# RG-LRU's shifted products handed out in finer steps, and the S5 scan started eight steps later, in a hybrid decoder block

## Chip, core and metric

The kernel runs on one core of a Trainium2 chip. The metric is the time of one execution on the device in microseconds. Three runs of the kernel before gave 1511.58, 1511.49 and 1508.52 us (median 1511.49). A fourth execution was profiled; all rows below come from it.

## What is computed

One layer of a decoder on 256 tokens with model width 2048, everything in float32. After an RMS norm one large product `xn @ w_in` feeds three branches that are merged by sigmoid gates, then comes `w_out`, a residual, a second norm, and an MLP of width 8192.

```python
proj = xn @ w_in                                  # 2048 x 11264
u_s5, u_lru, q, k, v, gate_logits = jnp.split(proj, offs, axis=-1)
gates = jax.nn.sigmoid(gate_logits + b_gate)
y_s5   = s5_branch(u_s5, ...)      # complex diagonal scan over time, GELU, GLU
y_lru  = rglru_branch(u_lru, ...)  # causal convolution of width 4, two block gates, real scan over time
y_attn = stick_breaking_attention(q, k, v)
merged = g_s5 * (y_s5 @ w_br_s5) + g_lru * (y_lru @ w_br_lru) + g_attn * (y_attn @ w_br_attn)
h = x + merged @ w_out
h = h + squared(relu(rms(h) @ w_up)) @ w_down;  return rms(h)
```

In the RG-LRU branch the convolution is `xc = b + sum_k x[t-3+k] * w[k]`: one scaled copy and three shifted products. In the S5 branch the complex scan is turned into real ones by rotating with a table of cosines and sines.

## The kernel before

**Units.** All weights (w_in, the three w_br, w_glu, w_out, w_up, w_down) are read once as a stream of 520 units. A unit is two 128x512 float32 pieces, 512 KB. SyncE loads it into a `raw` tile (L130, three buffers). ScalarE casts it to `hi` (L146), VectorE takes `lo = raw - hi` (L147), each with three buffers, and TensorE does three products per piece, hi by hi, lo by hi and hi by lo, so that fp32r products keep the precision. A unit is 12 matmuls of 512 columns in `chunk_tok` (L241 to L243) and `pair_tok`, or 24 of 256 columns in `chunk` (L225 to L227). I number the units from 0, and write cast k, lo k and raw k for the instructions that make unit k's tiles.

`next_unit` issues the loads to unit i+3 and cast and lo of unit i+2 ahead of the matmuls of unit i. With three buffers, cast k can start when unit k-3 has left TensorE, which is when unit k-2 starts there.

**Order of the units.** 0 to 15 and 16 to 31 are w_in for the inputs of RG-LRU and of S5 (24 matmuls each). 32 to 79 are four times eight units of gate columns and four of w_br_lru (from here 12 matmuls). 80 to 127 make k, q and v twice, 128 to 175 are gates and w_br_attn, 176 to 191 gates of S5, then w_glu, w_br_s5 with more gates, w_out, and from unit 264 the MLP.

**Side work.** Everything else (norm, convolution, scans, attention) is written as generators. After each unit's matmuls `pump` adds every task's rate to its credit and runs one step, up to a `yield`, for each whole credit. What a step issues is put in program order behind the casts, los and matmuls so far, on every engine that it uses. `finish(task)` runs a task to its end on the spot; the RG-LRU task is finished ahead of unit 40, the S5 task ahead of the GLU at unit 192.

The names that matter here:
- `lru_half` (L523): for each of its two parts and two channel tiles a scaled copy (L535, ScalarE) and three shifted products (L537, VectorE), then a `yield`; then block products on TensorE (L543, L544), sigmoids (L545, L546), tanh (L550), exp (L555), the root (L563), the scan (L570), and the split of the result (L572, L573). Rate 1.15 steps a unit (L576). `scaled` (L386) makes its inputs, and those of S5.
- `s5_scan` (L631), rate 1.27 (L593), started ahead of unit 32: `s5_tables` (L604 to L611) makes the angles and two sines with a table of ScalarE; `s5_split` (L618 to L623) splits an input tile into `ux`; `s5_stack` (L627) copies it with twelve small DMAs on SyncE's queue, the one on which the weights are loaded; then eight rounds of products (L650), copies (L652), rotations (L660 to L670, L681 to L692) and scans (L705).
- `gates` (L750, L751): VectorE scales the logits, ScalarE takes their sigmoid, which needs another table than the sine.

Of the kernel before, what the change touches and what calls it, by code (L numbers as in the profile page):

```python
# [46 lines left out]
def hybrid_block(ctx: ExitStack, tc: tile.TileContext, io, out):  # L47
# [116 lines left out]
    def later(gens, rate):  # L164
        side.append([deque(gens), rate, 0.0])
        return side[-1]
# [333 lines left out]
    def lru_load():  # L500
        for t, src in ((wr, "lru_w_r"), (wi, "lru_w_i")):
            for h in range(2):
                nc.sync.dma_start(t[h * 64:(h + 1) * 64, :, h * 64:(h + 1) * 64], io[src][h])
                yield

    def lru_params():
        for _ in range(4):
            yield
        lc = const.tile([P, 4, WT], F32, name="lc")
        nc.vector.scalar_tensor_tensor(lc[:, 0, :], lam, -1.0, lam, ALU.mult, ALU.min)  # L510
        nc.scalar.activation(lc[:, 1, :], lc[:, 0, :], AF.Exp)
        nc.scalar.activation(lc[:, 2, :], lc[:, 1, :], AF.Ln, bias=1.0)
        nc.vector.tensor_scalar(lc[:, 3, :], lam, -1.0, 0.0, ALU.mult, ALU.max)
        nc.vector.tensor_tensor(lc[:, 3, :], lc[:, 3, :], lc[:, 2, :], ALU.add)
        nc.vector.tensor_scalar(sp4, lc[:, 3, :], 4.0, None, ALU.mult)
        nc.vector.tensor_scalar(nsp8, lc[:, 3, :], -8.0, None, ALU.mult)
        yield
        yield from lru_load()
# [4 lines left out]
    def lru_half(c, us):  # L523
        parts = []
        for m in range(2):
            if m == 0:
                t = [lp.tile([P, 2, L], F32, tag=n_, name=f"lru_{n_}{c}") for n_ in ("xc", "r", "i", "th")]
            else:
                w4 = [pp.tile([P, 2, 2, L], F32, tag=n_, name=f"lru_{n_}{c}", bufs=2) for n_ in ("tc", "ts")]
                t = [w_[:, k] for w_ in w4 for k in range(2)]  # L530
            cts = [(j, slice(4 * c + 2 * m + j, 4 * c + 2 * m + j + 1)) for j in range(2)]
            parts.append((us[m], cts, *t))
        for u, cts, xc, r, i_, th in parts:
            for j, k in cts:
                nc.scalar.activation(xc[:, j, :], u[:, j, :], AF.Identity, scale=cw[:, 3, k], bias=cb[:, k])  # L535
                for s in range(1, 4):
                    nc.vector.scalar_tensor_tensor(xc[:, j, s:], u[:, j, :L - s], cw[:, 3 - s, k], xc[:, j, s:], ALU.mult, ALU.add)  # L537
                yield
        yield
        for u, cts, xc, r, i_, th in parts:  # L540
            for j, k in cts:
                ps = pss.tile([P, CH], F32, tag="ps", name=f"ps_l{c}_{k.start}")
                nc.tensor.matmul(ps[:, 0:L], wr[:, k.start, :], xc[:, j, :], start=True, stop=True, skip_group_check=True)  # L543
                nc.tensor.matmul(ps[:, L:], wi[:, k.start, :], xc[:, j, :], start=False, stop=True, skip_group_check=True)  # L544
                nc.scalar.activation(r[:, j, :], ps[:, 0:L], AF.Sigmoid, bias=br_[:, k])  # L545
                nc.scalar.activation(i_[:, j, :], ps[:, L:], AF.Sigmoid, bias=bi_[:, k])  # L546
            yield
        for u, cts, xc, r, i_, th in parts:
            for j, k in cts:
                nc.scalar.activation(th[:, j, :], r[:, j, :], AF.Tanh, scale=sp4[:, k])  # L550
            nc.vector.tensor_tensor(i_, i_, xc, ALU.mult)
        yield
        for u, cts, xc, r, i_, th in parts:
            for j, k in cts:
                nc.scalar.activation(r[:, j, :], r[:, j, :], AF.Exp, scale=nsp8[:, k])  # L555
        yield
        for u, cts, xc, r, i_, th in parts:
            nc.vector.scalar_tensor_tensor(th, r, 1.0, th, ALU.add, ALU.mult)
            nc.scalar.activation(r, th, AF.Identity, scale=-1.0, bias=1.0)
            nc.vector.scalar_tensor_tensor(th, r, 1.0, th, ALU.add, ALU.mult)  # L560
        yield
        for u, cts, xc, r, i_, th in parts:
            nc.scalar.activation(th, th, AF.Sqrt, bias=tiny)  # L563
        yield
        for u, cts, xc, r, i_, th in parts:
            nc.vector.tensor_tensor(i_, i_, th, ALU.mult)
        yield
        for u, cts, xc, r, i_, th in parts:
            for j, k in cts:
                nc.vector.tensor_tensor_scan(xc[:, j, :], r[:, j, :], i_[:, j, :], 0.0, ALU.mult, ALU.add)  # L570
            s = slice(cts[0][1].start, cts[0][1].start + 2)
            nc.scalar.copy(ylru_hi[:, s, :], xc)  # L572
            nc.vector.tensor_tensor(ylru_lo[:, s, :], xc, ylru_hi[:, s, :].bitcast(F32), ALU.subtract)  # L573
            yield

    lq = later([lru_params()], 1.15)  # L576
    u_banks = {}

    def lru_in(c):
# [10 lines left out]
    lru_in(1)  # L590


    S5_RATE = 1.27  # L593

    def s5_tables(b):
        c = pp.tile([P, NT, 16, 16], F32, tag="tc", name=f"tc{b}", bufs=2)
# [34 lines left out]
    def s5_scan():  # L631
        v = ypool.tile([P, 2, NT, L], F32, tag="yhi", name="s5_v")
        t12 = ypool.tile([P, 2, NT, L], F32, tag="ylo", name="s5_t")
        vr, vi, t1, t2 = v[:, 0], v[:, 1], t12[:, 0], t12[:, 1]
        tabs, more = s5_tables(0)
        yield from more
        s5_split(0)
        yield
        yield
        for t in range(NT):  # L640
            s5_stack(t)
            yield
        tt = nc.vector.tensor_tensor
        for b in range(WT):
            c, s = tabs
            t3 = pp.tile([P, NT, L], F32, tag="t3", name=f"t3_{b}")
            for t in range(NT):
                ps = pss.tile([P, CH], F32, tag="ps", name=f"ps_v{b}")
                for i in range(2):
                    nc.tensor.matmul(ps[:, i * L:(i + 1) * L], stk[:, t, 1, i * P:(i + 1) * P], stk[:, t, 0, :], start=i == 0, stop=True,  # L650
                                     skip_group_check=True)
                nc.scalar.copy(v[:, :, t, :], v2(ps))  # L652
                if t % 2:
                    yield
            more = iter(())
            if b + 1 < WT:
                s5_split(b + 1)
                tabs, more = s5_tables(b + 1)
                yield
            tt(t1, vr, c, ALU.mult)  # L660
            yield
            tt(t2, vi, s, ALU.mult)
            yield
            tt(t1, t1, t2, ALU.add)
            yield
            tt(t3, vi, c, ALU.mult)
            yield
            tt(vr, vr, s, ALU.mult)
            yield
            tt(t3, t3, vr, ALU.subtract)  # L670
            next(more, None)
            yield
            for x_ in (t1, t3):
                for t in range(NT):
                    j = b * NT + t
                    tt_scan(x_[:, t, :], rad[:, j:j + 1].broadcast_to([P, L]), x_[:, t, :])
                    if b + 1 < WT and x_ is t1:
                        s5_stack(t)
                    yield
            next(more, None)  # L680
            tt(t2, t1, c, ALU.mult)  # L681
            yield
            tt(vr, t3, s, ALU.mult)
            next(more, None)
            yield
            tt(t2, t2, vr, ALU.subtract)
            yield
            tt(vi, t3, c, ALU.mult)
            yield
            tt(t1, t1, s, ALU.mult)  # L690
            yield
            tt(t1, t1, vi, ALU.add)  # L692
            yield
            yield
            ps = pss.tile([P, CH], F32, tag="ps", name=f"ps_y{b}")
            for k, w_ in enumerate((t2, t1)):
                for t in range(NT):
                    nc.tensor.matmul(ps[t * 32:t * 32 + 32, 0:L], ce[:, k, b * NT + t, :, :], w_[:, t, :], start=k == 0, stop=k == 1,
                                     skip_group_check=True, tile_position=(0, t * 32))
            nc.vector.scalar_tensor_tensor(us5[:, b, :], us5[:, b, :], dsk[:, b:b + 1], ps[:, 0:L], ALU.mult, ALU.add)  # L700
            if b % 2:
                gq.append(later([gelu(b)], 1.0))
# [62 lines left out]
    def gate_branch(idx, wname, ys, ready):  # L765
        for c in range(4):
            gts = gates(idx, c, lambda c_, j: tmp.tile([P, 2, L], F32, tag="gate", name=f"gate{idx}_{c_}_{j}", bufs=3))
            finish(ready)
            branch(idx, c, gts, wname, ys)

    sq = later([s5_scan()], S5_RATE)
    gate_branch(1, "w_br_lru", lambda kt: (ylru_hi[:, kt, :], ylru_lo[:, kt, :]), ready=lq)
    lru.close()
# [98 lines left out]
    for q in range(4):  # L872
        s = slice(2 * q, 2 * q + 2)
# [4 lines left out]
    for c in range(2):  # L878
        banks = chunk("w_glu", c, W, lambda kt: (yg_hi[:, kt, :], yg_lo[:, kt, :]))
        for j in range(2):  # L880
# [4 lines left out]
            s = slice(c * 4 + 2 * j, c * 4 + 2 * j + 2)  # L885
# [285 lines left out]
```

## Time and profile before

| what | value |
|---|---|
| median of three runs | 1511.49 us |
| the profiled execution | 1512.1 us |
| its span, first to last instruction | 1510.3 us |
| TensorE (PE) | 1488.4 us busy (99%), 7518 matmuls |
| VectorE (DVE) | 1175.2 us busy (78%) |
| ScalarE (ACT) | 782.3 us busy (52%) |
| mean granted clock of TensorE | 0.995 |
| chain that ended last | PE 83%, DVE 9%, issue 3%, ACT 2%, DMA 2% |

How to read it: the ends of matmuls are modelled, and a matmul of 512 columns is shown for 0.39 us while the next one starts 0.23 us after it. Time that TensorE lost is therefore read from the distance between two starts, not from the busy share.

### The profile page before, as it was taken

What the parts mean: (1) busy time and instruction counts of PE and PEld (TensorE: products, weight loads), DVE (VectorE), ACT (ScalarE), POOL (GpSimd) and SP (SyncE); (2) the same over time, 40 slices, a digit from 0 to 9 for tenths busy, and PEclk for the clock granted to TensorE, in tenths of its full rate; (3) what the DMA queues carried; (4) which work ended last, traced back from release to release, by engine and by line L of the source; (5) the groups of instructions that cost most, each with busy time, mean ns of one, the idle gap of its engine ahead of it and who ended that gap; (6) DMA issues with size and microseconds to landing.
All of it is one profiled execution on the core that took longest, in us unless ns stands there. A gap on an engine that the chain in (4) does not pass through costs nothing.

```text
span 1510.3 us, 19900 instructions
## 1 busy us (share of the span) xinstructions
PE 1488.4 (99%) x7518; PEld 1260.5 (83%) x7518; DVE 1175.2 (78%) x1468; ACT 782.3 (52%) x920; POOL 35.3 (2%) x60
## 2 busy tenths in 40 slices
PE   9999999999999999999999999999999999999997
PEld 9997788989887878988887888888888888888886
DVE  6767998897988989689799796568854787558965
ACT  6767556565765564544455544344433444344443
POOL 1400000000000000000000000000000000000011
PEclk9999999999999999999999999999999999999999
DMA  9546766665555666666855666666666666666664
GB/s 287 157 153 176 228 205 201 187 182 168 175 172 183 208 182 210 189 202 190 276 182 188 197 184 205 194 185 196 198 194 193 193 195 195 195 191 191 192 197 152
DMA packets 89858, 292.41 MB, mean 194 GB/s; under 512 B 12834, under 2 KB 17058, under 8 KB 89634
## 3 DMA queue, kind: packets, MB, share of 16 engines
q1 hardware_dynamic: 89618, 291.07, 62.6%
q8 instruction: 59, 0.97, 0.3%
q14 instruction: 37, 0.30, 0.1%
q10 hardware_dynamic: 144, 0.07, 0.0%
HBM read 282.71 MB, written 2.10 MB: 189 GB/s over the span
## 4 chain that ended last, share of the span: by engine, by line
PE 83%; DVE 9%; issue 3%; ACT 2%; DMA 2%; SPq 0%; DVEq 0%; ACTq 0%
PE mt_w_up L242 6%; PE mt_w_up L241 6%; PE mt_w_up L243 6%; PE mt_w_in L242 5%; PE mt_w_in L243 5%; PE mt_w_in L241 5%; PE mt_w_down L242 4%; PE mt_w_down L241 4%; PE mt_w_down L243 4%; PE mp_w_down L277 4%; PE mp_w_down L278 4%; PE mp_w_down L276 4%; PE mm_w_in L227 4%; PE mm_w_in L225 4%; PE mm_w_in L226 4%; DVE lo L147 3%
## 5 line engine op out<-in xcount | busy, mean ns | idle before, releaser
L146 ACT CAST hi<-raw 128x1024 fp32r<-128x1024 f32 (+1 forms) x521 | 545.2, 1049 | 625.9 <-PE mt_w_up L243 131.4
L147 DVE TENSOR_TENSOR lo<-raw,hi 128x1024 fp32r<-128x1024 f32 (+1 forms) x521 | 637.9, 1225 | 287.7 <-ACT hi L146 284.1
L242 PE MATMUL mt_w_in<-lo,xhi 128*128 128x512 f32 x448 | 176.1, 393 | 3.9 <-DVE lo L147 3.7
L241 PE MATMUL mt_w_in<-hi,xhi 128*128 128x512 f32 x448 | 175.2, 396 | 0.2 <-ACT hi L146 0.2
L243 PE MATMUL mt_w_in<-hi,xlo 128*128 128x512 f32 x448 | 175.2, 391 | 0.0
L241 PE MATMUL mt_w_up<-hi,hhi 128*128 128x512 f32 x448 | 174.3, 389 | 0.0
L242 PE MATMUL mt_w_up<-lo,hhi 128*128 128x512 f32 x448 | 174.3, 389 | 0.0
L243 PE MATMUL mt_w_up<-hi,hlo 128*128 128x512 f32 x448 | 174.3, 389 | 0.0
L227 PE MATMUL mm_w_in<-xhi,lo 128*128 128x256 f32 x512 | 145.4, 286 | 4.5 <-DVE lo L147 4.5
L225 PE MATMUL mm_w_in<-xhi,hi 128*128 128x256 f32 x512 | 146.5, 286 | 0.5 <-ACT hi L146 0.4
L226 PE MATMUL mm_w_in<-xlo,hi 128*128 128x256 f32 x512 | 145.7, 285 | 0.0
L728 DVE STREAM_TRANSPOSE reluT<-relu 32x256 f32<-32x256 f32 x256 | 111.5, 436 | 4.2
L242 PEld LDWEIGHTS mt_w_in<-lo,xhi 128*128 128x128 f32 x448 | 84.6, 189 | 24.0 <-DVE lo L147 7.6
L227 PEld LDWEIGHTS mm_w_in<-xhi,lo 128*128 128x128 f32 x512 | 98.7, 194 | 5.5 <-DVE lo L147 5.5
L242 PE MATMUL mt_w_down<-lo,hd_hi 128*128 128x512 f32 (+1 forms) x272 | 102.5, 377 | 0.0
L241 PE MATMUL mt_w_down<-hi,hd_hi 128*128 128x512 f32 (+1 forms) x272 | 102.4, 377 | 0.0
L243 PE MATMUL mt_w_down<-hi,hd_lo 128*128 128x512 f32 (+1 forms) x272 | 102.4, 376 | 0.0
L225 PEld LDWEIGHTS mm_w_in<-xhi,hi 128*128 128x128 f32 x512 | 99.2, 194 | 1.1 <-ACT hi L146 1.0
L277 PE MATMUL mp_w_down<-lo,hd_hi 128*128 128x512 f32 x256 | 99.8, 390 | 0.1
L278 PE MATMUL mp_w_down<-hi,hd_lo 128*128 128x512 f32 x256 | 99.6, 389 | 0.0
L276 PE MATMUL mp_w_down<-hi,hd_hi 128*128 128x512 f32 x256 | 99.6, 389 | 0.0
L241 PEld LDWEIGHTS mt_w_in<-hi,xhi 128*128 128x128 f32 x448 | 84.5, 189 | 17.8 <-ACT hi L146 0.7
(299 smaller groups left out, 2370.2 us busy)
## 6 DMA issues: line engine op xcount, KB each, us to landing
raw<-in_w_in SPq DMA_DIRECT2D x175, 512.0 KB, 4.3
raw<-in_w_up SPq DMA_DIRECT2D x128, 512.0 KB, 4.2
raw<-in_w_down SPq DMA_DIRECT2D x128, 512.0 KB, 4.2
raw<-in_w_out SPq DMA_DIRECT2D x32, 512.0 KB, 4.2
raw<-in_w_br_lru SPq DMA_DIRECT2D x16, 512.0 KB, 4.6
raw<-in_w_br_attn SPq DMA_DIRECT2D x16, 512.0 KB, 4.1
raw<-in_w_br_s SPq DMA_DIRECT2D x16, 512.0 KB, 4.1
stk<-ux SPq DMA_DIRECT2D x96, 64.0 KB, 4.1
```

The source lines that it names most:

```text
L146: anchor["act"] = nc.scalar.copy(h[:, k, :], r[:, k, :]).ins
L147: anchor["dve"] = nc.vector.tensor_tensor(l_[:, k, :], r[:, k, :], h[:, k, :].bitcast(F32), ALU.subtract).ins
L225: nc.tensor.matmul(o, wh[:, kk, s], xh, start=first and ct % 2 == 0, stop=False, skip_group_check=True)
L226: nc.tensor.matmul(o, wh[:, kk, s], xl, start=False, stop=False, skip_group_check=True)
L227: mm = nc.tensor.matmul(o, wl[:, kk, s], xh, start=False, stop=last and ct % 2 == 1, skip_group_check=True)
L241: nc.tensor.matmul(banks[j], xh[:, s], wh[:, a:b], start=kt == 0, stop=False)
L242: nc.tensor.matmul(banks[j], xh[:, s], wl[:, a:b], start=False, stop=False)
L243: return nc.tensor.matmul(banks[j], xl[:, s], wh[:, a:b], start=False, stop=kt == ng * UK - 1)
L276: nc.tensor.matmul(o, xh[:, s], wh[:, kk, :], start=kt == 0, stop=False)
L277: nc.tensor.matmul(o, xh[:, s], wl[:, kk, :], start=False, stop=False)
L278: mm = nc.tensor.matmul(o, xl[:, s], wh[:, kk, :], start=False, stop=kt == ng * UK - 1)
L728: nc.vector.transpose(d_[32 * a:32 * a + 32, :, :, 32 * b:32 * b + 32], s_[32 * b:32 * b + 32, :, :, 32 * a:32 * a + 32])
```

## The change

```diff
--- before.py
+++ after.py
@@ -535,6 +535,8 @@
                 nc.scalar.activation(xc[:, j, :], u[:, j, :], AF.Identity, scale=cw[:, 3, k], bias=cb[:, k])
                 for s in range(1, 4):
                     nc.vector.scalar_tensor_tensor(xc[:, j, s:], u[:, j, :L - s], cw[:, 3 - s, k], xc[:, j, s:], ALU.mult, ALU.add)
+                    if s == 2:
+                        yield
                 yield
         yield
         for u, cts, xc, r, i_, th in parts:
@@ -573,7 +575,7 @@
             nc.vector.tensor_tensor(ylru_lo[:, s, :], xc, ylru_hi[:, s, :].bitcast(F32), ALU.subtract)
             yield
 
-    lq = later([lru_params()], 1.15)
+    lq = later([lru_params()], 1.45)
     u_banks = {}
 
     def lru_in(c):
@@ -590,7 +592,7 @@
     lru_in(1)
 
 
-    S5_RATE = 1.27
+    S5_RATE = 1.35
 
     def s5_tables(b):
         c = pp.tile([P, NT, 16, 16], F32, tag="tc", name=f"tc{b}", bufs=2)
@@ -632,6 +634,8 @@
         v = ypool.tile([P, 2, NT, L], F32, tag="yhi", name="s5_v")
         t12 = ypool.tile([P, 2, NT, L], F32, tag="ylo", name="s5_t")
         vr, vi, t1, t2 = v[:, 0], v[:, 1], t12[:, 0], t12[:, 1]
+        for _ in range(8):
+            yield
         tabs, more = s5_tables(0)
         yield from more
         s5_split(0)
```

Four things: a second `yield` inside the three shifted products of each of a half's four tiles (after the product with s = 2), so that a half has 18 steps in place of 14; the RG-LRU task's rate 1.45 in place of 1.15; the S5 task's rate 1.35 in place of 1.27; and eight empty steps ahead of the S5 task's first. No arithmetic is added or taken away. Every later step of both tasks falls at another unit. Line numbers after the first edit are 2 higher than before, after the last 4 higher.

VectorE around lo 26 (`lo_1120` before, `lo_1115` after): the last RG-LRU split of the first half, the products of the second (L537), and the scaled inputs of S5 (L386). Before:

```order
L573 TENSOR_TENSOR ylru_lo<-lru_tc_631,ylru_hi 128x512
L537 SCALAR_TENSOR_TENSOR lru_xc_1069<-ulru_817,par,lru_xc_1069 128x255 x2
L537 SCALAR_TENSOR_TENSOR lru_xc_1069<-ulru_817,par,lru_xc_1069 128x254 x2
L537 SCALAR_TENSOR_TENSOR lru_xc_1069<-ulru_817,par,lru_xc_1069 128x253 x2
L386 TENSOR_TENSOR us_99<-mm_w_in_0_16_821,rstd 128x512
L386 TENSOR_TENSOR us_99<-mm_w_in_1_16_822,rstd 128x512
L147 TENSOR_TENSOR lo_1120<-raw_1079,hi_1119 128x1024
```

After:

```order
L575 TENSOR_TENSOR ylru_lo<-lru_tc_631,ylru_hi 128x512
L537 SCALAR_TENSOR_TENSOR lru_xc_1099<-ulru_797,par,lru_xc_1099 128x255
L386 TENSOR_TENSOR us_99<-mm_w_in_0_16_801,rstd 128x512
L537 SCALAR_TENSOR_TENSOR lru_xc_1099<-ulru_797,par,lru_xc_1099 128x254
L386 TENSOR_TENSOR us_99<-mm_w_in_1_16_802,rstd 128x512
L147 TENSOR_TENSOR lo_1115<-raw_1069,hi_1114 128x1024
```

Ahead of lo 26 there were six products, and now there are two; the others stand behind lo 26, 27 and 28.

ScalarE at the S5 task's first sines (`ts`, `tc`), between two casts; before these are cast 37 (`hi_1485`) and cast 38:

```order
L146 CAST hi_1485<-raw_1458 128x1024
L572 CAST ylru_hi<-lru_xc_1069 128x512
L618 CAST ux<-us_99 128x256
L622 ACTIVATE ux<-bco,par 128x2x64
L609 ACTIVATE tc_1431<-ts_1432 128x1024
L622 ACTIVATE ux<-bco,par 128x2x64
L610 ACT_TABLE_LOAD
L610 ACTIVATE ts_1432<-ts_1432 128x1024
L572 CAST ylru_hi<-lru_tc_1073 128x512
L611 ACTIVATE tc_1431<-tc_1431,half_pi 128x1024
L146 CAST hi_1510<-raw_1483 128x1024
```

After, cast 42 (`hi_1581`) and cast 43; `gate_0_0` and `gate_0_1` are the gates of units 32 to 39:

```order
L146 CAST hi_1581<-raw_1551 128x1024
L620 CAST ux<-us_99 128x256
L624 ACTIVATE ux<-bco,par 128x2x64
L611 ACTIVATE tc_1548<-ts_1549 128x1024
L755 ACT_TABLE_LOAD
L755 ACTIVATE gate_0_0_1571<-gate_0_0_1571 128x512
L755 ACTIVATE gate_0_1_1574<-gate_0_1_1574 128x512
L612 ACT_TABLE_LOAD
L612 ACTIVATE ts_1549<-ts_1549 128x1024
L613 ACTIVATE tc_1548<-tc_1548,half_pi 128x1024
L624 ACTIVATE ux<-bco,par 128x2x64
L146 CAST hi_1608<-raw_1579 128x1024
```

The sines moved from unit 37 to unit 42, where the sigmoids of the first gates (L755) now stand among them with a table load of their own; RG-LRU's two casts (L572) are gone from there.

ScalarE at a later round of S5. Before, this stands between cast 150 (`hi_4654`) and cast 151, with the gates of w_br_attn's second chunk:

```order
L146 CAST hi_4654<-raw_4623 128x1024
L609 ACTIVATE tc_4380<-ts_4381 128x1024
L610 ACT_TABLE_LOAD
L610 ACTIVATE ts_4381<-ts_4381 128x1024
L751 ACT_TABLE_LOAD
L751 ACTIVATE gate_1_0_4644<-gate_1_0_4644 128x512
L751 ACTIVATE gate_1_1_4647<-gate_1_1_4647 128x512
L611 ACT_TABLE_LOAD
L611 ACTIVATE tc_4380<-tc_4380,half_pi 128x1024
L146 CAST hi_4676<-raw_4652 128x1024
```

After, between cast 78 (`hi_2420`) and cast 79, with the gates of w_br_lru's fourth chunk:

```order
L146 CAST hi_2420<-raw_2389 128x1024
L611 ACTIVATE tc_2174<-ts_2175 128x1024
L612 ACT_TABLE_LOAD
L612 ACTIVATE ts_2175<-ts_2175 128x1024
L755 ACT_TABLE_LOAD
L755 ACTIVATE gate_3_0_2410<-gate_3_0_2410 128x512
L755 ACTIVATE gate_3_1_2413<-gate_3_1_2413 128x512
L613 ACT_TABLE_LOAD
L613 ACTIVATE tc_2174<-tc_2174,half_pi 128x1024
L146 CAST hi_2442<-raw_2418 128x1024
```

The same ten instructions with three table loads now stand at unit 78. At unit 149 of the kernel after, sine, cosine and gates also meet, in an order with two table loads.

## Rows read from the trace of the kernel before

**Rows 1.** The page: a costly group; one DMA issue (xcount, KB, us to landing).
```profile
L147 DVE TENSOR_TENSOR lo<-raw,hi 128x1024 fp32r<-128x1024 f32 (+1 forms) x521 | 637.9, 1225 | 287.7 <-ACT hi L146 284.1
...
raw<-in_w_in SPq DMA_DIRECT2D x175, 512.0 KB, 4.3
```
**Rows 2.** Timeline of PE in the MLP: start us, us, instruction.
```profile
1200.10 0.39 PE L242 MATMUL mt_w_up<-lo,hhi 128*128 128x512 f32 x1
...
1200.33 0.39 PE L243 MATMUL mt_w_up<-hi,hlo 128*128 128x512 f32 x1
```
**Rows 3.** Timeline of PE: matmuls of units 14, 26, 32, 36, 151 that waited.
```profile
51.63 0.39 PE L227 MATMUL mm_w_in<-xhi,lo 128*128 128x256 f32 x1 [0.44 <-DVE lo L147]
...
92.31 0.42 PE L227 MATMUL mm_w_in<-xhi,lo 128*128 128x256 f32 x1 [1.93 <-DVE lo L147]
...
115.49 0.50 PE L242 MATMUL mt_w_in<-lo,xhi 128*128 128x512 f32 x1 [0.73 <-DVE lo L147]
...
129.18 0.50 PE L242 MATMUL mt_w_in<-lo,xhi 128*128 128x512 f32 x1 [1.91 <-DVE lo L147]
...
484.08 0.73 PE L241 MATMUL mt_w_br_attn<-hi,ya_hi 128*128 128x512 f32 x2 [2.15 <-ACT hi L146]
```
**Rows 4.** Windows: stretch, length, busy of PE, PEld, DVE, ACT, POOL, PEclk, DMA, GB/s.
```profile
92.60:96.00 3.40, 3.40 (x18) 3.40 (x18) 3.40 (x7) 0.00 (x0) 0.00 (x0) 0.51 0.74 182
...
485.10:488.50 3.40, 3.40 (x8) 2.72 (x9) 3.40 (x4) 0.83 (x1) 0.00 (x0) 0.51 0.51 154
1200.00:1203.40 3.40, 3.40 (x17) 2.82 (x16) 2.87 (x5) 1.50 (x2) 0.00 (x0) 1.00 0.65 188
```
**Rows 5.** Timeline of DVE ahead of lo 26.
```profile
84.57 1.27 DVE L570 TENSOR_TENSOR_SCAN lru_tc<-lru_tc,lru_ts 128x256 f32<-128x256 f32 x2
...
86.87 0.69 DVE L573 TENSOR_TENSOR ylru_lo<-lru_tc,ylru_hi 128x512 fp32r<-128x512 f32 x1
87.47 2.45 DVE L537 SCALAR_TENSOR_TENSOR lru_xc<-ulru,par,lru_xc 128x255 f32<-128x255 f32 x6
89.84 1.29 DVE L386 TENSOR_TENSOR us<-mm_w_in,rstd 128x512 f32<-128x512 f32 x2
91.04 1.22 DVE L147 TENSOR_TENSOR lo<-raw,hi 128x1024 fp32r<-128x1024 f32 x1
```
**Rows 6.** Timeline of ACT from cast 150 to cast 151.
```profile
473.81 1.06 ACT L146 CAST hi<-raw 128x1024 fp32r<-128x1024 f32 x1 [0.49 <-PE mt_w_in L243]
474.77 1.05 ACT L609 ACTIVATE tc<-ts 128x1024 f32<-128x1024 f32 x1
475.84 1.28 ACT L610 ACT_TABLE_LOAD   x1
477.13 1.06 ACT L610 ACTIVATE ts<-ts 128x1024 f32<-128x1024 f32 x1
478.20 1.28 ACT L751 ACT_TABLE_LOAD   x1
479.50 1.15 ACT L751 ACTIVATE gate<-gate 128x512 f32<-128x512 f32 x2
480.65 1.28 ACT L611 ACT_TABLE_LOAD   x1
481.95 1.15 ACT L611 ACTIVATE tc<-tc,half_pi 128x1024 f32<-128x1024 f32 x1
483.00 2.92 ACT L146 CAST hi<-raw 128x1024 fp32r<-128x1024 f32 x3
```
**Rows 7.** Timeline of ACT: casts 31 and 32; the first copy into ux.
```profile
103.85 1.05 ACT L146 CAST hi<-raw 128x1024 fp32r<-128x1024 f32 x1
...
112.92 2.93 ACT L146 CAST hi<-raw 128x1024 fp32r<-128x1024 f32 x3
...
127.17 0.40 ACT L618 CAST ux<-us 128x256 fp32r<-128x256 f32 x1
```
**Rows 8.** Timeline of SyncE's queue: three stack copies.
```profile
133.72 1.90 SPq L627 DMA_DIRECT2D stk<-ux  x3
```

## The prediction, made before the changed kernel ran
> **What bounds the kernel now.** I read the page first. TensorE is busy all the time, so time can only go where it waits, and VectorE's costliest group, the 521 los, stood idle for 284 us for casts [rows 1]: a lo follows its cast, and a matmul follows both. Next I took the timeline of PE in the MLP for the undisturbed pace: 0.227 us between two starts of 512 columns, so 12 x 0.227 = 2.72 us a unit [rows 2]; the channel units take 24 x 0.12 = 2.88. Then I looked for starts that are later than that. The reader should see five waits, four for a lo and one for a cast [rows 3]. What a wait costs is the idle time shown plus about 0.16 us, since the shown end of the matmul ahead lies past the pace (0.39 against 0.227, [rows 2]). After the three longest, the windows view shows the granted clock at 0.51, the 1.2 GHz level, for a stretch of 3.4 us, with 8 matmuls where 17 fit [rows 4]. That is half of 3.4, less what other waits would have taken: 1.6 us each time.
>
> So the five cost: unit 14, 0.44 + 0.16 = 0.6; unit 26, 2.1 + 1.6 = 3.7; unit 32, 0.9; unit 36, 2.1 + 1.6 = 3.7; unit 151, 2.3, 0.8 more for its lo, and 1.6, so 4.7. Together 13.6 us. Later starts of under 0.7 us each in units 25 to 170 add, by my estimate, 4 us. All lie where the RG-LRU and S5 tasks run, so the change can touch nearly all of them, and the MLP not at all.
>
> **The rule behind the waits.** Cast k can start when unit k-2 starts on TensorE. It takes 1.05 us, the lo about 1.2, and TensorE wants them after two units. So if ScalarE has other work between two casts, from the start of the one to the start of the next an interval I, and the first of them begins d after its unit k-2, the next unit waits for its hi by d + I + 1.05 - 8.16 (three units of 2.72). Test it: casts 150 and 151 start at 473.81 and 483.00, I = 9.19 [rows 6]; with d = 0.2 that gives 2.28, and 2.3 was measured [rows 3].
>
> **The change, part by part.**
>
> *Finer products, unit 14.* Before, six products stood ahead of lo 14, now one; the wait of 0.6 goes.
>
> *Finer products, units 23 to 26.* Before lo 26 VectorE had a 0.6 us split, six products at 0.40 and two scaled inputs at 0.6, 4.2 us, and TensorE waited [rows 5, 3]. In the order after, four products of those six stand behind lo 26, 27 and 28. But the whole half now runs two units later, and its last part is as dense as before. I went through the order after by hand with the durations of [rows 5] (512 columns 0.6, a pair of scans 1.2, a lo 1.13). Cast 23 comes out at about 78.8 on this trace's clock, after two table loads. Lo 23 is ready at 80.0, 0.1 late. Then five pieces of 0.6 (a ce block, two L568, two scans) put lo 24 at 84.2, 1.3 late; four pieces put lo 25 at 87.75, 0.7 late; two products, a split and two scaled inputs put lo 26 at 91.5, 0.85 late. So 3.0 us in place of 3.7, in four waits too short for the clock to fall. Ends: 1.5 if cast 23 comes a microsecond sooner, 4.6 if the clock falls once. I take 3.0.
>
> *Units 32 to 38.* The casts of the second half's sigmoids and exponentials moved from units 30 and 31 to 32 and 33. The interval of 9.07 between casts 31 and 32 [rows 7] now ends in front of unit 34, where units are 2.72 and not 2.88 long: the wait is 1.4 in place of 0.9. The long wait of unit 36 goes: before, the scan, S5's angles and the split for br_lru met there; now S5 begins six units later (8 / 1.35), and I find only 0.3 at units 37 and 38. So 1.7 in place of 4.6.
>
> *S5's first sines, unit 42.* This is given back here. The block between casts 42 and 43 is cast 0.96, L611 1.07, load 1.29, two sigmoids 1.15, load 1.3, sine 1.07, cosine 1.05 [rows 6], and three short pieces at 0.3 [rows 7]: I = 8.8. Cast 42 follows another piece of S5 (L608) and raw 42, which lands 4.3 us after its buffer is free [rows 1], so d is 0.2 to 1.05, and I take 1.05. The wait for hi is 1.05 + 8.8 + 1.05 - 8.16 = 2.75, the lo adds 1.05: 3.8. All three waits of over 2 us lost the clock, so I add it with three chances in four, 1.2. Sum 5.0; the ends are 2.7 and 5.4. Before, the block at unit 37 met a TensorE that had just waited, and cost nothing of its own.
>
> *Units 78 and 149.* The ten instructions of [rows 6] now stand at unit 78, with the same neighbours on VectorE. Same wait, 2.3 + 0.8, and the clock with three in five: 4.1. At unit 149 sine, cosine and gates meet again with one load fewer: I = 9.19 - 1.29 = 7.9, wait 1.0 + 0.8 = 1.8, with no fall of the clock. So 5.9 in place of 4.7.
>
> Of the clock, the rows show two levels and a fall after each wait of 2.1 to 2.3 us [rows 3, 4]. The Trainium skill (TensorE: Matmul & The Clock Gate, Part 1: The HAM clock gate) says that the window the chip looks at runs freely and does not start with the kernel; by it the same wait at another place may keep the clock. The trace cannot show that, since all three lost it. Without that rule I would add 1.6 at units 42 and 78 in full, 1.0 us more in the sum.
>
> *Small late starts.* S5's work no longer lies beside the first w_br_lru units, but a few of its steps meet the attention stage otherwise (around unit 107 VectorE's work piles up more, around 143 as before). I take 2.5 in place of 4, with ends at 1 and 5.
>
> S5 ends at unit 186 in place of 190; there it was not waited for, so that is worth nothing.
>
> **The sum.** Before 13.6 + 4 = 17.6. After 3.0 + 1.7 + 5.0 + 5.9 + 2.5 = 18.1. The difference is +0.5 on the profiled execution's 1512.1 us, which lies 0.6 above the median of the runs. On the scale of the runs: 1511.5 + 0.5 = 1512.0. A measurement of this kernel can tell about 0.2%, 3 us, from no change.
>
> **The rivals.**
>
> *Faster: the new blocks are better covered than I think.* If cast 42 starts at once (d = 0.2), the clock holds at units 42 and 78, and units 23 to 26 take the lower end, then units 42, 78 and 23 to 26 cost 2.7, 3.1 and 1.5: 2.3 + 1.0 + 1.5 = 4.8 us less than in my sum, so 1507.2. For it: before, the block at unit 37 vanished in another wait. Against it: nothing waits just ahead of units 43 and 79 now, and the block of [rows 6] cost its full price in an even stretch.
>
> *Slower: SyncE's queue.* The twelve stack copies of S5's first tile wait for `ux`, whose last piece is now the end of the block at unit 42, about 146 us. Three stand ahead of raw 46, six ahead of raw 47, three ahead of raw 48, at 0.63 us each [rows 8]. Raw 47 is then issued at about 152.5 and lands at 157, and lo 47 has some 1.4 us to spare. From a delay of 1.4 us on, each further one is paid in full, and the raws after it wait in the same queue; with 3 us late, about 1515. For it: nothing else is as late in that queue. Against it: the stretch has just waited 5 us at unit 43, which lets the loads catch up.
>
> *Only the gain.* If the moves were worth what they take away and the table loads were hidden as ScalarE's 52% suggests, the time would be 17.6 - 3.0 - 1.7 - 4.0 = 9 us less, 1502.6. Rows 6 speak against it.
>
> **Chances.** My sum (1509 to 1515): 0.47. The better covered blocks (1504 to 1509): 0.26. SyncE's queue or the clock falling everywhere (1515 to 1519): 0.23. Only the gain: 0.04. For the range of 8 in 10 I go from 1505 to 1517; the likeliest case alone spans 1509 to 1515. Faster by over 0.2% is the second and fourth case, 0.30; within it 0.46; slower 0.24.
>
> **What would show it.** In the profile after: no wait at unit 14, none of over 2 us at units 26 and 36; a cast interval of near 8.8 us ahead of unit 43 with TensorE waiting 3 to 4 us for hi and lo; one of 9.2 us ahead of unit 79; one of 7.9 ahead of unit 150. Stretches at half clock near units 43 and 79 in place of those at 92, 130 and 485 us. I am wrong if units 43 and 79 start on time, if units 23 to 26 lose the clock, or if waits appear after unit 100 that I did not place.

## The result and the profile after

The changed kernel took 1516.79 us (median of five runs, 1515.88 to 1517.14); the kernel before, run beside it, 1511.31 (five runs). The ratio is 1.0036, with a 95% interval of 1.0024 to 1.0047: slower by 5.5 us, where the prediction said 0.5 slower with a range to 1517, so the time lies 0.2 us inside the range's upper end. The profiled execution's span is 1515.4 us, against 1510.3.

The busy times have not moved (PE 1488.0, DVE 1176.3, ACT 782.5 us), so only waits can differ. The start of a unit on PE shows where:

| start of unit, us | before | after | after minus before |
|---|---|---|---|
| 40 | 141.84 | 135.32 | -6.5 |
| 62 | 206.33 | 202.92 | -3.4 |
| 84 | 269.40 | 275.04 | +5.6 |
| 192 | 604.12 | 608.56 | +4.4 |
| 400 | 1174.71 | 1179.70 | +5.0 |

The gain came, 6.5 us by unit 40, and between units 40 and 84 twelve were lost. The timeline of PE after, its matmuls that waited (start, length, instruction, idle time ahead and what ended it):

```profile
84.15 0.39 PE L227 MATMUL mm_w_in<-xhi,lo 128*128 128x256 f32 x1 [0.70 <-DVE lo L147]
87.88 0.39 PE L227 MATMUL mm_w_in<-xhi,lo 128*128 128x256 f32 x1 [0.59 <-DVE lo L147]
91.60 0.39 PE L227 MATMUL mm_w_in<-xhi,lo 128*128 128x256 f32 x1 [0.58 <-DVE lo L147]
...
118.85 0.51 PE L242 MATMUL mt_w_in<-lo,xhi 128*128 128x512 f32 x1 [0.52 <-DVE lo L147]
...
145.85 0.73 PE L241 MATMUL mt_w_br_lru<-hi,ylru_hi 128*128 128x512 f32 x2 [2.21 <-ACT hi L146]
...
159.71 0.50 PE L242 MATMUL mt_w_in<-lo,xhi 128*128 128x512 f32 x1 [0.53 <-DVE lo L147]
...
180.33 0.50 PE L242 MATMUL mt_w_br_lru<-lo,ylru_hi 128*128 128x512 f32 x1 [1.03 <-DVE lo L147]
200.30 0.50 PE L242 MATMUL mt_w_in<-lo,xhi 128*128 128x512 f32 x1 [0.76 <-DVE lo L147]
...
256.12 0.73 PE L241 MATMUL mt_w_br_lru<-hi,ylru_hi 128*128 128x512 f32 x2 [2.90 <-ACT hi L146]
...
486.17 0.73 PE L241 MATMUL mt_w_br_attn<-hi,ya_hi 128*128 128x512 f32 x2 [1.46 <-ACT hi L146]
```

These answer to [rows 3]: unit 14's wait is gone, units 24 to 26 wait three times for 0.6 to 0.7, unit 32's now stands at unit 34 (118.85), unit 36's is gone, unit 151's now stands at unit 150 (486.17), and new ones stand at units 43 (145.85), 47 (159.71), 54 (180.33), 61 (200.30) and 79 (256.12). The windows view after (columns as in [rows 4]):

```profile
146.00:149.40 3.40, 3.18 (x13) 2.32 (x14) 3.40 (x4) 1.70 (x2) 0.00 (x0) 1.00 0.50 129
...
258.10:261.50 3.40, 3.40 (x10) 2.68 (x9) 3.40 (x4) 0.00 (x0) 0.00 (x0) 0.53 0.52 154
```

After unit 43's wait the granted clock stays at 1.00, the 2.4 GHz level; after unit 79's it falls to 1.2 GHz. That is the only such stretch while TensorE still has work, in place of the three before.

ScalarE at the block ahead of unit 79, which answers to [rows 6]:

```profile
244.82 1.06 ACT L146 CAST hi<-raw 128x1024 fp32r<-128x1024 f32 x1
246.79 1.06 ACT L611 ACTIVATE tc<-ts 128x1024 f32<-128x1024 f32 x1 [0.92 <-DVE ts L609]
247.87 1.28 ACT L612 ACT_TABLE_LOAD   x1
249.17 1.06 ACT L612 ACTIVATE ts<-ts 128x1024 f32<-128x1024 f32 x1
250.24 1.28 ACT L755 ACT_TABLE_LOAD   x1
251.53 1.15 ACT L755 ACTIVATE gate<-gate 128x512 f32<-128x512 f32 x2
252.69 1.28 ACT L613 ACT_TABLE_LOAD   x1
253.98 1.15 ACT L613 ACTIVATE tc<-tc,half_pi 128x1024 f32<-128x1024 f32 x1
255.03 1.98 ACT L146 CAST hi<-raw 128x1024 fp32r<-128x1024 f32 x2
```

The same ten instructions, but an interval of 10.21 in place of 9.19: L611 waits 0.92 for VectorE's L609.

SyncE's queue around raw 46 (issued at 147.08) and raw 47 (152.66), which answers to [rows 8]:

```profile
144.89 2.04 SPq L629 DMA_DIRECT2D stk<-ux  x3
147.08 0.48 SPq L130 DMA_DIRECT2D raw<-in_w_in  x1
147.60 4.95 SPq L629 DMA_DIRECT2D stk<-ux  x6
152.66 0.53 SPq L130 DMA_DIRECT2D raw<-in_w_in  x1
```

VectorE ahead of lo 54 (179.06):

```profile
173.75 1.22 DVE L147 TENSOR_TENSOR lo<-raw,hi 128x1024 fp32r<-128x1024 f32 x1
174.89 1.22 DVE L674 TENSOR_TENSOR t<-t,s_v 128x1024 f32<-128x1024 f32 x1
176.02 1.22 DVE L606 TENSOR_TENSOR tc<-fhi,flo 128x1024 f32<-128x1024 f32 x1
177.16 0.69 DVE L709 TENSOR_TENSOR_SCAN s_t<-rad,s_t 128x256 f32<-128x256 f32 x1
177.76 1.39 DVE L754 SCALAR_TENSOR_TENSOR gate<-mt_w_in,rstd_tok,gb 128x512 f32<-128x512 f32 x2
179.06 1.22 DVE L147 TENSOR_TENSOR lo<-raw,hi 128x1024 fp32r<-128x1024 f32 x1
```

Five instructions stand between lo 53 (173.75) and lo 54, 4.2 us from the start of the first to lo 54, with VectorE never idle; unit 54 lost 1.33. Before, it started on time.

### The profile page after: what moved, and what is told of

It reads as the page before. It is cut to its first block, busy times and chain, and to the rows that moved or that the text cites. A ratio compares the mean times of both kernels' runs of the same rounds, so it can differ in the third digit from the quotient of the medians.

```text
span 1515.4 us, 19902 instructions
## 1 busy us (share of the span) xinstructions
PE 1488.0 (98%) x7518; PEld 1256.9 (83%) x7518; DVE 1176.3 (78%) x1468; ACT 782.5 (52%) x920; POOL 35.0 (2%) x60
## 4 chain that ended last, share of the span: by engine, by line
PE 71%; DVE 15%; ACT 5%; issue 5%; DMA 4%; SPq 1%; DVEq 0%; ACTq 0%
PE mt_w_up L242 6%; PE mt_w_up L243 6%; PE mt_w_up L241 6%; DVE lo L147 6%; PE mt_w_down L242 4%; PE mt_w_down L241 4%; PE mp_w_down L277 4%; PE mt_w_down L243 4%; PE mp_w_down L278 4%; PE mp_w_down L276 4%; PE mt_w_in L242 4%; PE mt_w_in L241 3%; PE mt_w_in L243 3%; PE mm_w_in L227 3%; PE mm_w_in L225 3%
## 5 line engine op out<-in xcount | busy, mean ns | idle before, releaser
L242 PEld LDWEIGHTS mt_w_in<-lo,xhi 128*128 128x128 f32 x448 | 84.2, 188 | 24.1 <-DVE lo L147 7.5
```

The lines of the kernel that those rows point to most:

```text
L242: nc.tensor.matmul(banks[j], xh[:, s], wl[:, a:b], start=False, stop=False)
```

## The experiments

My theory after the result: ScalarE's and VectorE's blocks of S5 meet the gates (L754, L755), and on which units they meet is set by the count of empty steps. Rivals: the finer products cost something themselves; a later start is bad in itself; SyncE's queue did it.

**One part alone.** `e1_lru_only` keeps the second yield and 1.45, `e2_s5_only` the eight steps and 1.35.

```diff
-    S5_RATE = 1.35                       # these four lines: e1
+    S5_RATE = 1.27
-        for _ in range(8):
-            yield
...
-                    if s == 2:           # these four: e2
-                        yield
-    lq = later([lru_params()], 1.45)
+    lq = later([lru_params()], 1.15)
```

> Only the RG-LRU part of the change (second yield, rate 1.45); the S5 task as in the kernel before. Theory A (the loss is made by where S5's steps fall: its sines between gate sigmoids on ScalarE, its los' neighbours on VectorE, its stack copies on SyncE's queue): the waits of units 23 to 26 as in the changed kernel (2.7 us), the wait at unit 34 (1 us), but S5's angles and split still meet RG-LRU's end, with cast intervals of about 6.5 us at units 36 and 37 in a row, some 4 to 5 us lost there; unit 151 loses its 4.7 us as before. Sum about 1510, 1508 to 1513. Rival B (the finer steps themselves cost, since a half runs two units later and as dense as before): 1514 or more, waits in units 20 to 40 above those of the kernel before.

> Only the S5 part of the change (eight empty steps, rate 1.35); RG-LRU as in the kernel before. Theory A: the waits of units 26 and 32 stay (4.6 us), the one at unit 36 goes (4 us gained), and the whole loss of units 43, 47, 54, 61, 70 to 72, 79 and 150 appears as in the changed kernel: about 1518, 1516 to 1520, slower than the changed kernel by about 1 to 2 us. Rival B: the S5 part costs nothing, about 1511 or less.

e1: 1510.87, ratio 0.9995 (0.9987 to 1.0004). e2: 1517.37, ratio 1.0040 (1.0026 to 1.0053). The whole loss is with the S5 part. The RG-LRU part alone changes nothing that can be measured: with S5 still starting at unit 32, its second half meets S5 at units 33 to 38, where TensorE sits idle for 4.4 us in six waits. So the rival that the finer products cost something themselves falls.

**The gates' table loads.** `e3_gate_copy` takes them away beside w_br_lru (a copy there, the sigmoid left out), `e8_probe_loads` adds two to one block of ten steps.

```diff
-            nc.scalar.activation(g, g, AF.Sigmoid)       # e3
+            nc.scalar.activation(g, g, AF.Copy if idx == 1 else AF.Sigmoid)
...
+            if b == 1:                                   # e8, between sine and cosine
+                for k in range(2):
+                    nc.scalar.activation(probe[:, k:k + 1], half_pi, AF.Sigmoid)
+                    nc.scalar.activation(probe[:, 2 + k:3 + k], half_pi, AF.Sin, scale=0.5)
```

> The changed kernel with a copy in place of the sigmoid for the gates of w_br_lru alone (the sigmoid is left out there), so that no table load for them stands among S5's sines: the interval ahead of unit 43 falls from 8.8 to 7.5 us, that ahead of unit 79 from 10.2 to about 5.2. Theory A: unit 79 loses under 0.5 us in place of 5.8, unit 43 about 2 in place of 3, unit 150 as in the changed kernel: about 1510, 1508.5 to 1512. Rival C (VectorE is late there anyway, and the table loads only fill its time): no gain beyond 1.5 us, 1515.5 or more.

> The kernel with ten empty steps, and at one place, the second round's sines at unit 62, four activations of one column each (two sigmoids and two sines, written to a tile that nothing reads), so that three table loads stand in that block in place of one: interval about 8.7 us in place of 5.4. Theory A: wait for hi of 0.2 + 8.7 + 1.05 - 8.16 = 1.8 at unit 63 and 1.0 for its lo, so 2.8, and 1.6 more if the clock falls: 1504 to 1505.5. Rival F (the loads hide in ScalarE's idle time, and what cost in the changed kernel was something else at those places): 1501 to 1502.

e3: 1509.92, 6.9 less than after. The wait of unit 79 is gone. But a part of the gain was lost again at unit 54, which lost 4.5 in place of 1.3. TensorE waited 2.87 us there, and the one fall of the clock in this run came with it. The cast that it waited for (179.12) had itself waited 1.44 us for its weights to land:

```profile
180.21 1.22 PE L241 MATMUL mt_w_in<-hi,xhi 128*128 128x512 f32 x2 [2.87 <-ACT hi L146]
```

e8: 1506.06, 5.0 more than ten steps without the probe (1501.10), and a little above the 1504 to 1505.5 expected. In its trace, two of the three loads, PE's wait for the cast behind them (the last load, an activation of 0.20 and the cosine), and a window behind it:

```profile
198.68 1.28 ACT L616 ACT_TABLE_LOAD   x1
...
200.18 1.28 ACT L617 ACT_TABLE_LOAD   x1
201.47 0.20 ACT L617 ACTIVATE probe<-half_pi 128x1 f32<-128x1 f32 x1
...
202.62 1.98 ACT L146 CAST hi<-raw 128x1024 fp32r<-128x1024 f32 x2
```
```profile
203.70 0.73 PE L241 MATMUL mt_w_in<-hi,xhi 128*128 128x512 f32 x2 [2.47 <-ACT hi L146]
```
```profile
204.50:207.90 3.40, 3.25 (x10) 2.53 (x11) 3.40 (x4) 1.05 (x2) 0.00 (x0) 0.66 0.48 151
```

An interval between casts of 9.02 (193.60 to 202.62) made a wait of 2.5 where ten steps had none, and the clock fell behind it, part of the way through the window shown (0.66). So a block's length does cause the wait; this is shown by adding it, not only by taking it away.

**The count of empty steps.** `e7_nine_steps`, `e4_ten_steps`, `e11_eleven_steps` and `e12_twelve_steps` (rate 1.35) differ from after in one line, `e5_one_step` in the rate (1.27) as well:

```diff
-        for _ in range(8):
+        for _ in range(10):
```

> The changed kernel with ten empty steps in place of eight, nothing else. By the order of its instructions no gate sigmoid stands among S5's sines any more: the longest cast intervals after unit 40 are 6.4 us (units 44, 133) and the rest 5.4. Theory A: the losses at units 43, 79 and 150 (11.8 us together) shrink to about 3, the small waits of units 44 to 77 stay at about 5: about 1508, 1506 to 1511, faster than the kernel before. Rival D (what costs is that S5 starts later and runs at a higher rate, on VectorE): 1516 to 1518, as the changed kernel.

> RG-LRU as in the changed kernel, S5 at the old rate 1.27 with one empty step in place of eight. By its order no gate sigmoid stands among S5's sines; the longest cast intervals after unit 34 are 6.5 (unit 138), 5.8 and 5.5. Theory A (the cast interval sets the price, whatever the start and the rate): against the kernel with only the RG-LRU part (1510.9) the 3.5 us at unit 151 go and some 1.5 us at units 36 to 38: about 1506, 1503.5 to 1508. Rival D (a late start or a high rate is what matters): as the kernel with only the RG-LRU part, 1510 to 1511.5, since the start moves by less than one unit.

> The changed kernel with nine empty steps. By its order one block of three table loads with gates among the sines (cast interval 9.1) is left, at unit 150; units 43 and 79 have intervals of 6.4 and 5.4. Theory A: as the kernel with ten steps (1501.1) and 3.5 to 4.7 us more at units 150 to 152: about 1505, 1504 to 1507. Rival D (start and rate matter): between eight and ten steps, the time lies between 1516.8 and 1501.1 by the start alone, about 1509.

> Eleven empty steps, the whole computation. In the order ScalarE's longest blocks from unit 34 on are 6.7 us with two loads (unit 98) and 6.2 (units 122, 134), so theory A gives the time of ten steps, 1500 to 1503. Rival L, ten is one lucky meeting among many: 1507 to 1513, with new stalls at units that had none.

> Twelve empty steps, the whole computation. In the order there are blocks of 7.5 us with three loads at unit 100 and of 8.8 us with four at unit 126, both in the v units, where casts have 6 to 8 us to spare; so theory A, taken with the room a cast has at each place, gives 1500 to 1504. If the length of the block decided alone, two more waits of 1 to 2.5 us with a fall of the clock: 1505 to 1508. Rival L: 1507 to 1513.

| empty steps | median, us | ratio to before (95%) |
|---|---|---|
| 1 (rate 1.27) | 1505.77 | 0.9963 (0.9950 to 0.9975) |
| 8 (after) | 1516.79 | 1.0036 (1.0024 to 1.0047) |
| 9 | 1515.59 | 1.0033 (1.0021 to 1.0046) |
| 10 | 1501.10 | 0.9932 (0.9920 to 0.9945) |
| 11 | 1507.47 | 0.9971 (0.9961 to 0.9982) |
| 12 | 1524.03 | 1.0082 (1.0068 to 1.0096) |

The time jumps by up to 17 us from one count to the next. Ten and eleven steps start S5 later than after does and are faster, so a later start is not bad in itself. One step came out as expected. Ten steps beat both kernels; I had expected 1508, and for nine 1505. Eleven came out at 1507.5, at the lower edge of what I wrote for a lucky ten, and not at theory A's 1500 to 1503. Ten steps' first sines, casts 44 and 45:

```profile
141.43 1.03 ACT L146 CAST hi<-raw 128x1024 fp32r<-128x1024 f32 x1
...
147.64 1.03 ACT L146 CAST hi<-raw 128x1024 fp32r<-128x1024 f32 x1
```

The interval is 6.21, where after it was 8.67; TensorE waited 0.15 for the cast. Twelve was a plain miss of mine. I had placed its long ScalarE blocks in the v units and judged that casts have room there. Against ten steps it loses 8.9 us more in units 100 to 104 and 6.3 more at unit 127. ScalarE's rows there, first twelve steps, then ten:

```profile
303.68 1.28 ACT L817 ACT_TABLE_LOAD   x1
...
307.00 1.28 ACT L612 ACT_TABLE_LOAD   x1
...
312.52 1.28 ACT L801 ACT_TABLE_LOAD   x1
...
314.77 1.28 ACT L802 ACT_TABLE_LOAD   x1
```
```profile
300.96 1.28 ACT L817 ACT_TABLE_LOAD   x1
...
305.22 0.53 ACT L801 ACTIVATE s<-s 128x384 f32<-128x384 f32 x1
305.78 0.53 ACT L802 ACTIVATE s<-s 128x384 f32<-128x384 f32 x1
```

The attention task loads one table ahead (L817) for its exponentials (L801) and logarithms (L802). In ten steps S5's sines stand ahead of that load, and L801 and L802 need none of their own. In twelve the sine's load (L612) stands between, and from there on exponentials and logarithms each have loads of their own, in both halves of the attention: 15 at these two lines, where ten steps has none, and 49 loads in the whole trace against 32. My expectation weighed these blocks by the room that casts have, and not by what they do to VectorE. Cast 127 had 2.1 us to spare; VectorE had none. VectorE's rows in twelve steps, with lo 127 (420.15), and the matmul that waited:

```profile
419.01 0.56 DVE L803 SCALAR_TENSOR_TENSOR s<-z,s 128x384 f32<-128x384 f32 x1 [3.05 <-ACT s L802]
...
420.15 1.22 DVE L147 TENSOR_TENSOR lo<-raw,hi 128x1024 fp32r<-128x1024 f32 x1
```
```profile
421.43 0.65 PE L242 MATMUL mt_w_in<-lo,xhi 128*128 128x512 f32 x1 [4.44 <-DVE lo L147]
```

VectorE stands idle in front of an attention piece (L803) that waits for ScalarE's loads, and lo 127 stands behind it in the queue. Of unit 127's 6.3, 4.6 are that wait; behind it the granted clock was 0.52 for 3.4 us (421.50 to 424.90), the 1.2 GHz level. That the loads make the 15.2 us is read from this trace; no run takes them away.

**Nine against ten.** What makes 14 us between them?

```diff
+            nc.scalar.activation(g, g, AF.Copy if idx > 0 else AF.Sigmoid)
```

> Nine empty steps, and the gates of both attention branches (idx 1 and 2) copied instead of taken through a sigmoid; the sigmoid is left out. It takes ScalarE's table loads for those gates away, and nothing else in the order. Theory A, what decides is how often ScalarE has three loads between two casts: nine steps lost some 5.5 us at units 150 to 153, 2.7 at units 43 and 44 and 2 to 3 at units 62 and 80, all with a gate's load in the block; without them 1506 to 1508, and within 7 us of ten steps with the same copies. Rival D, that nine and ten steps differ by VectorE's pile-ups (units 54, 142, 143, 157): 1511 to 1513, and ten steps with the same copies stay 11 us or more ahead.

> Ten empty steps, and the same copies in place of the gates' sigmoids (left out). Theory A: ten steps have no block with three loads from unit 34 on, so little is left to gain, the stalls at units 64, 82 and 153: 1497 to 1500. Rival D: 1497 to 1500 as well; what tells the two apart is the distance to nine steps with the copies, under 7 us by A, 11 or more by D.

e9: 1502.61, 13.0 less than nine steps and more than theory A had asked. e10: 1504.70, 3.6 more than ten. That e10 came out above 1500 was expected by neither theory. The distance of 14.5 became -2.1, so the loads, with the order that they bring, carry it, and the rival of VectorE's pile-ups falls: unit 54 still loses 1.4 in e9 (2.1 in nine steps). It is not their number alone: the traces hold 34 loads in nine steps, 32 in ten and 24 in each of the runs with copies. What differs is how many stand between two casts. One thing in my expectation was wrong. The copies do change the order, since the build arranges neighbouring instructions of an engine by itself, and with the gates copied the sine's table stays, so its loads go as well. The two runs do not part the one from the other. Unit starts in the four traces:

| start of unit, us | nine | ten | nine, copies | ten, copies |
|---|---|---|---|---|
| 40 | 135.31 | 134.97 | 135.62 | 135.75 |
| 62 | 202.67 | 197.77 | 197.87 | 201.67 |
| 84 | 270.19 | 262.60 | 262.86 | 266.49 |
| 128 | 413.97 | 406.48 | 406.58 | 410.37 |
| 192 | 607.50 | 592.45 | 593.94 | 597.03 |

Nine lost its 14 us in three places that hold gates (4.6 by unit 62, 2.7 by unit 84, 7.6 after 128). That e10 is slower than ten seems to have a reason of its own, in SyncE's queue with the copies (read from the traces, not tested by a run):

```profile
148.01 5.11 SPq L629 DMA_DIRECT2D stk<-ux  x6
153.22 0.53 SPq L130 DMA_DIRECT2D raw<-in_w_in  x1
```

In ten steps the same six copies start at 144.41: there the last piece of `ux` (L624) came ahead of the first sine, at 143.93, and here, by that changed order, behind both sines, at 147.30. Units 45 to 50 then lose 4.3 us, against 2.0 in ten steps and 1.0 in e9, whose copies began at 141.78.

**SyncE's queue.** `e6_stack_pool` puts the stack copies on another queue.

```diff
-            nc.sync.dma_start(stk[i * 32:...], w_[...])
+            nc.gpsimd.dma_start(stk[i * 32:...], w_[...])
```

> The changed kernel with S5's stack copies issued by GpSimd in place of SyncE. Theory A: raw 46 and raw 47 are issued when their buffers are free and no longer behind three and six copies, so cast 47 no longer starts late and the 1.2 us at unit 47 (with 0.4 at unit 46) go; units 43, 54, 61, 79 and 150 stay: about 1515.3, 1513.5 to 1516.5. Rival E: the loads are late because their buffers come free late, and the queue costs nothing: unit 47 waits as before, 1516.3 or more.

1520.42, ratio 1.0064 (1.0050 to 1.0078): slower than after by 3.6, a miss. In its place the edit did what was meant: raws 46 to 50 go out from 147.26 on with no copy among them, and from the start of unit 44 to that of 49 it takes 14.63 us in place of 15.88. So the queue cost after 1.25. But unit 43's wait was now 2.53 in place of 2.21, and the clock fell:

```profile
146.03 1.22 PE L241 MATMUL mt_w_br_lru<-hi,ylru_hi 128*128 128x512 f32 x2 [2.53 <-ACT hi L146]
```
```profile
146.20:149.60 3.40, 3.40 (x9) 2.46 (x10) 3.30 (x3) 1.67 (x2) 3.40 (x7) 0.52 0.61 135
```

That took the 1.25 back; the rest was lost in small waits at units 54 to 61, and one of 1.29 at unit 160 (519.98), which I have not traced to a cause.

## Why the prediction was near, and which step failed

| step, us lost | predicted | measured after |
|---|---|---|
| units 23 to 26 | 3.0 | 2.65 |
| units 32 to 38 | 1.7 | 1.6 |
| unit 43 | 5.0 | 3.0 |
| units 79 and 150 | 5.9 | 8.8 |
| small late starts | 2.5 | 7.3 |
| sum | 18.1 | 23.3 |

Measured is each unit's time beyond 2.72 or 2.88 us (2.88 also for k and q, units 80 to 95 and 104 to 119, which have 24 matmuls), less S5's own matmuls where a round has them there. Against the 17.6 before, 23.3 is 5.7 more; the spans differ by 5.0 (1515.37 and 1510.35).

**What held.** The three late los of units 24 to 26 came within 0.1 us of the times worked out by hand (84.10, 87.82 and 91.54 against 84.2, 87.75 and 91.5), and none made the clock fall. The rule of the cast interval held three times: unit 43, 0.77 + 8.67 + 1.05 - 8.16 = 2.33, measured 2.37; unit 79, 0.20 + 10.21 + 1.05 - 8.16 = 3.30, measured 3.34; in ten steps 1.03 + 6.21 + 1.05 - 8.16 = 0.13, measured 0.15.

**Sizes that were off.** At unit 43 the forecast took d = 1.05 and a likely fall of the clock; d was 0.77 and the clock held, so 3.0. At units 78 to 81 it was 5.8 in place of 4.1: cast 78 and cast 79 have "the same neighbours on VectorE" in the order, but L609 ran late behind a scan and lo 77, so the interval was 1.02 longer; and the clock, which I had priced at three chances in five, did fall. Units 149 to 152 lost 3.0 in place of 1.8: the interval ahead of unit 150 was 8.50 (476.59 to 485.09) and not 7.9.

**The step that failed** is "Small late starts", where the prediction says "I take 2.5 in place of 4": 7.3 were measured, beyond its upper end of 5. The order after puts S5's long pieces beside the first gate columns, and there I looked only at ScalarE's blocks that I had named. Missed were VectorE's block ahead of lo 54 (1.3), one sine block with L611 waiting 0.93 ahead of unit 61 (1.15), smaller ones at units 63, 70, 72, 143, 167 and 169 (3.6), and SyncE's queue (1.3). That last one was my rival: raw 47 was issued at 152.66 where I had worked out 152.5, and its cast began at 157.35 where I had said that it lands at 157. It paid 1.25, not 3, since it was only just too late. One small wait past unit 100, at unit 167 (0.6), is of the kind that the prediction named as a sign of being wrong.

That the time lies in the range, 0.2 us inside its end, is in part luck. The prediction's likeliest case, 1509 to 1515, did not come, and of the causes that it gave for 1515 to 1519, a late queue or the clock falling everywhere, little did: the queue cost 1.25 and the clock fell once. The errors partly cancelled: unit 43 came 2.0 under the forecast, units 79 and 150 and the small late starts 7.7 over it.

**What stays open.** With the S5 start as the only change, the times run from 1501 to 1524. Which count is good comes from where some ten blocks meet the gates and the attention. My reckoning from the order got one step right and the probe nearly, ten in its direction only, and eight's size, nine, eleven, twelve and the times of both runs with copies wrong; so it is shown that a long block between two casts makes the wait, but there is no rule that picks the count without a run. Eleven's 6.4 us over ten are spread over many units and were not traced to a cause. How much of the cost of the loads is the order that they bring was not separated.

## What to carry to other kernels

Before moving a long side task against a tight stream, list for each unit what stands between two casts and between two los on both engines, with table loads and the waits between the two engines, look whether another table comes between a table's load and its use, and price every interval by the rule that the trace gives; an average share of busy time (ScalarE 52%) says nothing. Where the start of such a task is a free number, try the neighbours of it: here two steps more turned a loss of 5.5 us into a gain of 10. And look at what a shared DMA queue holds behind a waiting copy.

## What the runs showed of the hardware

A wait of much the same length can end with the clock lowered or not. Unit 151's of 2.15 us before [rows 3] lowered it, as did 2.47 in e8 and 2.53 in e6; 2.21 after (146.00, above) did not. Nor did the wait of 2.15 at the same unit 151 in e1, where no stretch at the 1.2 GHz level stands while TensorE has work, and this one in one step, with its window:

```profile
129.83 0.50 PE L242 MATMUL mt_w_in<-lo,xhi 128*128 128x512 f32 x1 [2.20 <-DVE lo L147]
```
```profile
130.30:133.70 3.40, 3.27 (x15) 2.37 (x14) 3.34 (x7) 3.39 (x4) 0.00 (x0) 1.00 0.71 209
```

In e2 the order is even turned round: the clock held after the wait of 2.93 at unit 79 and fell after one of 1.15 at unit 150 (and 0.53 for its lo):

```profile
258.13 0.73 PE L241 MATMUL mt_w_br_lru<-hi,ylru_hi 128*128 128x512 f32 x2 [2.93 <-ACT hi L146]
...
487.22 0.73 PE L241 MATMUL mt_w_br_attn<-hi,ya_hi 128*128 128x512 f32 x2 [1.15 <-ACT hi L146]
```
```profile
258.00:261.40 3.40, 3.05 (x14) 2.27 (x15) 3.29 (x3) 1.98 (x3) 0.00 (x0) 1.00 0.27 77
...
489.20:492.60 3.40, 3.40 (x10) 2.63 (x9) 3.40 (x4) 0.00 (x0) 0.00 (x0) 0.51 0.75 199
```

The Trainium skill (TensorE: Matmul & The Clock Gate, Part 1: The HAM clock gate) says that the window looked at runs freely and does not start with the kernel; by it a wait's place matters beside its length, and these rows agree. A table load cost its 1.28 us and hardly more: in the block of unit 79 the activation starts 0.01 to 0.02 us after each load ends.
